# A two-layer decoder trunk: when a held feature pair's operands are made, and where the adding DMAs stand

## The chip, the cores and the metric

The kernel runs on one core of one Trainium2 chip. The metric is the device time of one execution in microseconds (us); lower is better. The program is written with a scheduler that decides the order of each engine's instructions by priorities and its own estimates, except where the code pins an instruction with `tc.keep_in_program_order`. Five engines take part: TensorE (PE, its weight loads PEld), VectorE (DVE), ScalarE (ACT), GpSimd (POOL) and the sync engine (SP). Each works its own list of instructions in order. DMAs are issued from SP's list (plain loads) and from POOL's list (loads that add to what already stands in the tile).

## The reference, cut to what matters

Two layers, each an attention mixer and a gated MLP, on a sequence of 512 tokens, width 1024, MLP width 2816 (22 features of 128):

```python
for layer in range(DEPTH):
    h = rms_norm(x, g_mix[layer])
    qkv = h @ w_in[layer]
    ...
    x = x + mix @ w_out[layer]
    h2 = rms_norm(x, g_ffn[layer])
    x = x + conv_gated_mlp(h2, w_up[layer], conv_w[layer], conv_b[layer], w_down[layer])
return rms_norm(x, g_final)

def conv_gated_mlp(h, w_up, conv_w, conv_b, w_down):
    u = causal_depthwise_conv(h @ w_up, conv_w, width=3) + conv_b
    gate, val = jnp.split(u, 2, axis=-1)
    return (jax.nn.silu(gate) * val) @ w_down
```

The change touches only the MLP's down projection, `(silu(gate) * val) @ w_down`, and what prepares its operands.

## The kernel before, in words

Every product is made of float32r parts: an operand is split into a rounded part (`whi`, cast by ACT) and the rest (`wlo`, subtracted by DVE), and PE makes three products of the parts. A list `units` (built before the layers run) names every weight tile in the order of use. `emit_dma` issues a unit's loads into raw buffers (5 of them), `emit_split` makes `whi` and `wlo` of it, and `use` hands a unit to the products and lets splits and loads run ahead as far as the buffers go.

The MLP runs over features of 128 columns. `up_pair(f)` is the gate and value up projection of feature f (PE tiles `upg` and `upv`, 24 matmuls each), followed by the convolution (ACT and DVE), SiLU and the product of the two, a page of 512 tokens. The down projection of features 0 to 17 is not made directly but by Winograd's form of Strassen's scheme, in three folds of three feature pairs each (`FOLDS`); features 18 to 21 go plainly (`PLAIN`). For that, sums and differences of both operands are needed:

- of the activations: `operands(g0, g1, qa)`, for a pair of features. Four 128x256 sums on POOL (tiles `s12` and `s34`, shown as `s`), then casts on ACT and subtractions on DVE into `ga` and `gs`.
- of `w_down`: a unit of kind `s1` loads two raw tiles `r0` and `r1` and a tile `tt` from SP, and POOL then adds further blocks of the weights by DMA: one of 256 KB onto half of `r0`, one of 512 KB onto all of `tt`, one of 256 KB onto half of `tt`. The three are issued together in `emit_dma` (L240 to L242), and the third adds onto bytes that the second has just written, so it waits for the second to land. When the unit is split, `emit_split` issues a fourth one (L277, 256 KB, onto half of `tt`), whose result is the unit of kind `s2`.

`fold(pairs)` makes the products: `p1` and `p5` of pair 0 and of pair 1 (they read `r0`), `p7` and `p6` of both (they read `tt`), then `p1`, `p6`, `p7`, `p5` of pair 2, then the products of the `s2` units, pair by pair. Each product is 6 matmuls, into the tiles `dx`, `dz`, `dw` and `dy`. So the first matmul that reads pair 2's `tt` is the first one of its `p6`, and this one comes right behind pair 2's `p1`.

Around the folds stands the loop at L1067:

```python
held = None
for f0, n in FOLDS:
    pairs = [pair_of(*held)] if held else []
    for f in range(f0 + 2 * len(pairs), f0 + n, 2):
        ...
    held = up_pair(f0 + n), up_pair(f0 + n + 1, HOLD_PRIO)
    fold(pairs)
```

The two features behind a fold (`held`) are projected before the fold, so that the fold's weights have time. Their operands (`pair_of`) are made at the head of the next fold's turn. In a layer this happens twice, behind the first and the second fold; behind the third the held features go to the plain part, which needs no such operands. Nothing pins the loads into `tt` on SP, nor the adding DMAs on POOL: their tiles are free early (three buffers, shared with a tile of attention), so the scheduler has pulled the `tt` loads and the two `tt` adds ahead, for the first fold of a layer into that layer's attention, for the other two to the end of the fold before.

Of the kernel before, what the change touches and what calls it, by code (L numbers as in the profile page):

```python
# [15 lines left out]
OP = mybir.AluOpType  # L16
# [47 lines left out]
def kernel(  # L64
# [21 lines left out]
    nc = tc.nc  # L86
# [37 lines left out]
    def bank(name, dtype=F, shape=(128, 512)):  # L124
        side = name in SIDE
        return pp.tile(list(shape), dtype, name=name, tag="side" if side else "main",
                       bufs=SIDE_BANKS if side else 8 - SIDE_BANKS)
# [80 lines left out]
    def raw_tile(shape=(128, 2, 512)):  # L208
        return sb.tile(list(shape), F, name="raw", tag="raw", bufs=RAW_BUFS)

    def emit_dma(force=False):
        u = n_dma[0]
        if u >= len(units) or (not force and n_raw[0] + RAWS[units[u][0]] > RAW_BUFS):
            return False
        n_dma[0] += 1
        kind, w, l, a, pieces = units[u]
        n_raw[0] += RAWS[kind]
        if kind == "t":
            k0, n = a
            raw = raw_tile()  # L220
            o = 0
            for c0, nc_ in pieces:
                nc.sync.dma_start(
                    out=raw[:, 0:n, o:o + nc_],
                    in_=w[l, k0 * 128:(k0 + n) * 128, c0:c0 + nc_].rearrange("(k p) c -> p k c", p=128))
                o += nc_
        elif kind == "f":
            raw = raw_tile((128, KD, 128))
            nc.sync.dma_start(out=raw, in_=w[l, :, a:a + 128].rearrange("(k p) c -> p k c", p=128))
        elif kind == "s1":  # L230
            raw = [raw_tile() for _ in range(2)]
            r0, r1 = raw
            tt = sb.tile([128, 2, 512], F, name="tt", tag="qkst", bufs=WIDE)


            b = w[l, a * 128:(a + 2) * 128, :].rearrange("(k p) (c n) -> p k c n", k=2, c=2)
            nc.sync.dma_start(out=r0, in_=b[:, 0])
            nc.sync.dma_start(out=tt, in_=b[:, 0])
            nc.sync.dma_start(out=r1, in_=b[:, 1])
            nc.gpsimd.dma_start(out=r0[:, 1], in_=b[:, 0, 0], accum_op=OP.add)  # L240
            nc.gpsimd.dma_start(out=tt, in_=b[:, :, 1], accum_op=OP.add)
            nc.gpsimd.dma_start(out=tt[:, 0], in_=b[:, 1, 1], accum_op=OP.add)  # L242
            raw = r0, r1, tt
        else:
            raw = None
        raws[u] = raw
        return True

    def hi_lo(src, shape=(128, 2, 512), n=None):
        hi = sb.tile(list(shape), FR, name="whi", tag="whi", bufs=HL_BUFS)  # L250
        lo = sb.tile(list(shape), FR, name="wlo", tag="wlo", bufs=HL_BUFS)
        n = n or shape[1]
        A.copy(hi[:, 0:n], src)
        V.tensor_tensor(out=lo[:, 0:n], in0=src, in1=hi[:, 0:n], op=OP.subtract)
        return hi, lo

    def emit_split():
        u = n_split[0]
        if u >= len(units):
            return  # L260
        while n_dma[0] <= u:
            emit_dma(True)
        n_split[0] += 1
        raw = raws.pop(u)
        kind, _, l, a, _ = units[u]
        with tc.high_priority(PRIO if u > 3 else 0):
            if kind == "t":
                split[u] = hi_lo(raw[:, 0:a[1]], n=a[1])
                n_raw[0] -= 1
            elif kind == "f":  # L270
                split[u] = hi_lo(raw, (128, KD, 128))
                n_raw[0] -= 1
            elif kind == "s1":
                r0, r1, tt = raw
                split[u] = hi_lo(r0), hi_lo(tt)

                nc.gpsimd.dma_start(out=tt[:, 0], in_=w_down[l, (a + 1) * 128:(a + 2) * 128, 0:512], accum_op=OP.add)  # L277
                kept[l, a] = r1, tt
                n_raw[0] -= 1
            else:  # L280
                r1, tt = kept.pop((l, a))
                split[u] = hi_lo(r1), hi_lo(tt[:, 0:1], n=1)
                n_raw[0] -= 1
        while emit_dma():
            pass
# [99 lines left out]
    for i, s in enumerate((lambda_q1, lambda_k1, lambda_q2, lambda_k2)):  # L385
        nc.sync.dma_start(out=lam_in[:, i, :],
                            in_=bass.AP(tensor=s.tensor, offset=s.offset, ap=[[0, 128], [1, DEPTH * 32]]))
    gd = const.tile([128, DEPTH], F, name="gd")
    for l in range(DEPTH):
        for h in range(2):  # L390
            nc.sync.dma_start(out=gd[64 * h:64 * h + 64, l:l + 1],
                                in_=g_diff[l:l + 1, :].rearrange("a p -> p a"))
# [187 lines left out]
    def act_h(k):  # L580
        return hT["hi"][k // 4][:, k % 4, :], hT["lo"][k // 4][:, k % 4, :]
# [345 lines left out]
    def mlp(l, nxt):  # L927
# [17 lines left out]
        def up_pair(f, prio=0):  # L945

            if f == 0:
                wts = use(4, 0)
                bs = [bank("up") for _ in range(4)]
                for i in range(2):  # L950
                    for g in range(4):
                        wh, wl = wts[g]
                        for k in range(KD):
                            ah, al = act_h(k)
                            sl = slice(256 * i, 256 * i + 256)
                            three_f(bs[g][:, sl], wh[:, k, :], wl[:, k, :], ah[:, sl], al[:, sl],
                                    k == 0, k == KD - 1)
                        now[0] += 2.6
                        if i == 0 and g in (1, 2):
                            hT_of(1 + g)  # L960
                        if i == 1:
                            emit_split()
                table_set(SILU)
                first.update({0: bs[0:2], 1: bs[2:4]})
            if f in first:
                bg, bv = first.pop(f)
            else:
                bg = feat_group("upg")
                bv = feat_group("upv")
            with tc.high_priority(prio):  # L970
                cg, cvl = conv((bg, bv), f)
            act(cg, cg, AF.Silu)
            V.tensor_tensor(out=cvl, in0=cg, in1=cvl, op=OP.mult)
            return cvl
# [87 lines left out]
        def pair_of(g0, g1):  # L1062
            qa = sb.tile([128, 8, 256], FR, name="ga", tag="quad", bufs=QUADS)
            parts(qa, 0, 1, g0[:, 0:256])
            return operands(g0, g1, qa)

        held = None  # L1067
        for f0, n in FOLDS:
            pairs = [pair_of(*held)] if held else []
            for f in range(f0 + 2 * len(pairs), f0 + n, 2):  # L1070
                qa = sb.tile([128, 8, 256], FR, name="ga", tag="quad", bufs=QUADS)
                g0 = up_pair(f)
                parts(qa, 0, 1, g0[:, 0:256])
                g1 = up_pair(f + 1)
                pairs.append(operands(g0, g1, qa))
            held = up_pair(f0 + n), up_pair(f0 + n + 1, HOLD_PRIO)
            fold(pairs)

        gh, gl = quad("gh"), quad("gl")
        f0, n = PLAIN  # L1080
# [120 lines left out]
```

## Time and profile before

| | |
|---|---|
| median of 3 runs | 1273.32 us (1272.75 to 1274.54) |
| the profiled execution, its own time | 1275.58 us |
| its span, first to last instruction | 1273.8 us |
| granted TensorE clock over the span, 1 is full speed | 0.991 |
| PE busy | 1220.1 us (96%), 5888 matmuls |
| DVE, ACT, POOL busy | 901.1, 672.7, 361.2 us |
| DMA: from SP's and the hardware's queue, from POOL's adding queue | 119.17 MB, 24.04 MB |

PE is busy nearly throughout, and every matmul of 512 columns starts 0.23 us after the one before when nothing is in the way. So time is read from the places where PE's next matmul starts later than that. An engine's idle time elsewhere costs nothing by itself.

### The profile page before, as it was taken

The numbers are of one execution on the slowest core, as the hardware profiler recorded it, in microseconds if no ns is written. First come the engines' busy times: TensorE is split into PE (matmuls) and PEld (weight loads), VectorE is DVE, ScalarE is ACT, GpSimd is POOL, SyncE is SP. The second block draws the span as 40 slices with busy tenths as digits, with TensorE's granted clock in tenths as the row PEclk, the third lists the DMA queues.
The fourth block names the chain that finished last, engine by engine and source line by source line (L and its number), as shares of the span: only waits on it lengthen the run. The fifth ranks groups of instructions, "written<-read, shape, count | busy, mean of one in ns | idle before, by whom it ended". The sixth has DMA issues, their size and how long they took to land. (4 is left out here: it accounts for less than half of the span.)

```text
span 1273.8 us, 16609 instructions
## 1 busy us (share of the span) xinstructions
PE 1220.1 (96%) x5888; PEld 991.7 (78%) x5888; DVE 901.1 (71%) x1619; ACT 672.7 (53%) x1224; POOL 361.2 (28%) x388
## 2 busy tenths in 40 slices
PE   6999899999999999999997999999999999999997
PEld 5877777789887887888885777878888878878885
DVE  6888878576668668568675768774776776675774
ACT  4767777544443443444463747783454444434444
POOL 3021335131125225223212114441212333332213
PEclk9999999999999999999999999999999999999999
DMA  6561112233447647745318121122244595585421
GB/s 224 159 150 50 60 58 66 69 90 93 113 107 194 153 112 177 179 100 142 97 46 207 55 82 56 61 70 67 84 116 111 136 210 122 127 205 131 99 83 67
DMA packets 157828, 144.27 MB, mean 113 GB/s; under 512 B 6826, under 2 KB 125648, under 8 KB 157744
## 3 DMA queue, kind: packets, MB, share of 16 engines
q1 hardware_dynamic: 144800, 119.17, 30.9%
q0 software_dynamic: 12944, 24.04, 11.9%
q8 instruction: 46, 0.75, 0.2%
q14 instruction: 38, 0.31, 0.1%
HBM read 141.09 MB, written 2.10 MB: 112 GB/s over the span
## 5 line engine op out<-in xcount | busy, mean ns | idle before, releaser
L99 DVE TENSOR_TENSOR wlo<-raw,whi 128x1024 fp32r<-128x1024 f32 x196 | 257.5, 1316 | 122.9 <-ACT whi L99 121.4
L99 ACT CAST whi<-raw 128x1024 fp32r<-128x1024 f32 x196 | 204.2, 1049 | 150.1 <-PE upg L99 39.6
L99 PE MATMUL upg<-hTh,whi 128*128 128x512 f32 x320 | 126.8, 396 | 6.4 <-ACT whi L99 6.4
L99 PE MATMUL upg<-hTh,wlo 128*128 128x512 f32 x320 | 127.1, 397 | 2.1 <-DVE wlo L99 2.1
L99 PE MATMUL upg<-hTl,whi 128*128 128x512 f32 x320 | 126.3, 395 | 0.0
L99 PE MATMUL upv<-hTh,whi 128*128 128x512 f32 x320 | 124.5, 389 | 0.0
L99 PE MATMUL upv<-hTl,whi 128*128 128x512 f32 x320 | 124.5, 389 | 0.0
L99 PE MATMUL upv<-hTh,wlo 128*128 128x512 f32 x320 | 124.5, 389 | 0.0
L99 POOL TENSOR_SCALAR p<-p,sm 128x512 f32<-128x512 f32 (+3 forms) x128 | 79.3, 630 | 154.1 <-PE sc L99 70.7
L99 ACT ACTIVATE p<-p,sm 128x512 f32<-128x512 f32 (+3 forms) x160 | 89.2, 559 | 45.8 <-DVE sm L99 44.7
L99 POOL TENSOR_TENSOR hn<-x,gbc 128x512 f32<-128x512 f32 x39 | 53.2, 1376 | 174.7 <-ACT hn L99 168.3
L99 PEld LDWEIGHTS upg<-hTh,whi 128*128 128x128 f32 x320 | 61.2, 191 | 20.6 <-ACT whi L99 8.1
L99 PEld LDWEIGHTS upg<-hTh,wlo 128*128 128x128 f32 x320 | 61.2, 191 | 16.6 <-DVE wlo L99 3.9
L99 ACT ACTIVATE cg<-cg 128x512 f32<-128x512 f32 x44 | 27.8, 632 | 86.4 <-DVE cg L99 86.3
L99 POOL TENSOR_TENSOR s<-cv 128x256 f32<-128x256 f32 x36 | 34.7, 982 | 135.9 <-DVE cv L99 135.9
L99 DVE TENSOR_TENSOR wlo<-tt,whi 128x1024 fp32r<-128x1024 f32 (+1 forms) x36 | 45.0, 1251 | 39.4 <-ACT whi L99 39.2
L99 PEld LDWEIGHTS upg<-hTl,whi 128*128 128x128 f32 x320 | 61.2, 191 | 12.9
L99 PEld LDWEIGHTS upv<-hTh,whi 128*128 128x128 f32 x320 | 60.1, 188 | 12.5
L99 PEld LDWEIGHTS upv<-hTl,whi 128*128 128x128 f32 x320 | 60.1, 188 | 12.5
L99 PEld LDWEIGHTS upv<-hTh,wlo 128*128 128x128 f32 x320 | 60.0, 188 | 12.5
L99 DVE SCALAR_TENSOR_TENSOR cv<-upv,conv,cv 128x511 f32<-128x511 f32 x80 | 59.7, 746 | 1.4
L99 DVE SCALAR_TENSOR_TENSOR cg<-upg,conv,cg 128x511 f32<-128x511 f32 x80 | 59.7, 746 | 1.4
(234 smaller groups left out, 3104.2 us busy)
## 6 DMA issues: line engine op xcount, KB each, us to landing
raw<-in_w_up_dram SPq DMA_DIRECT2D x88, 512.0 KB, 4.0
raw<-in_w_down_dram SPq DMA_DIRECT2D x44, 512.0 KB, 4.3
raw<-in_w_in_dram SPq DMA_DIRECT2D x40, 512.0 KB, 3.9
tt<-in_w_down_dram SPq DMA_DIRECT2D x18, 512.0 KB, 4.6
tt<-in_w_down_dram POOLq DMA_DIRECT2D x18, 512.0 KB, 9.1
tt<-in_w_down_dram POOLq DMA_DIRECT2D x36, 256.0 KB, 4.1
raw<-in_w_out_dram SPq DMA_DIRECT2D x16, 512.0 KB, 3.5
raw<-in_w_down_dram POOLq DMA_DIRECT2D x18, 256.0 KB, 4.1
```

What stands on the lines that cost most here:

```text
L99: i = f(*a, **k)
```

## The change

Three edits, all in the MLP's preparation.

1. The held pair's operands are made one step later: behind the up projection of the next fold's first own feature, not ahead of it. The loop covers the same features.
2. The load of `tt` on SP is kept in program order, so it stands between the loads of `r0` and `r1` of its unit.
3. The adding DMAs are no longer issued in `emit_dma`. They are put on a list in two stages for each unit, the first with the adds onto `r0` and onto all of `tt`, the second with the add onto half of `tt`. Each later `emit_split` issues one stage, and all stages that the unit to be split still needs. All adding DMAs, the fourth one too, are kept in program order on POOL.

```diff
             nc.sync.dma_start(out=r0, in_=b[:, 0])
-            nc.sync.dma_start(out=tt, in_=b[:, 0])
+            tc.keep_in_program_order(nc.sync.dma_start(out=tt, in_=b[:, 0]))
             nc.sync.dma_start(out=r1, in_=b[:, 1])
-            nc.gpsimd.dma_start(out=r0[:, 1], in_=b[:, 0, 0], accum_op=OP.add)
-            nc.gpsimd.dma_start(out=tt, in_=b[:, :, 1], accum_op=OP.add)
-            nc.gpsimd.dma_start(out=tt[:, 0], in_=b[:, 1, 1], accum_op=OP.add)
+            adding.append((u, [(r0[:, 1], b[:, 0, 0]), (tt, b[:, :, 1])]))
+            adding.append((u, [(tt[:, 0], b[:, 1, 1])]))
...
+    def add_now(dst, src):
+        tc.keep_in_program_order(nc.gpsimd.dma_start(out=dst, in_=src, accum_op=OP.add))
+
+    def add_some(u):
+
+        some = True
+        while adding and (some or adding[0][0] <= u):
+            some = False
+            for dst, src in adding.popleft()[1]:
+                add_now(dst, src)
...
         n_split[0] += 1
+        add_some(u)
         raw = raws.pop(u)
...
-                nc.gpsimd.dma_start(out=tt[:, 0], in_=w_down[l, (a + 1) * 128:(a + 2) * 128, 0:512], accum_op=OP.add)
+                add_now(tt[:, 0], w_down[l, (a + 1) * 128:(a + 2) * 128, 0:512])
...
         for f0, n in FOLDS:
-            pairs = [pair_of(*held)] if held else []
-            for f in range(f0 + 2 * len(pairs), f0 + n, 2):
+            pairs = []
+            for f in range(f0 + (2 if held else 0), f0 + n, 2):
+                g0 = up_pair(f)
+                if held:
+                    pairs.append(pair_of(*held))
+                    held = None
                 qa = sb.tile([128, 8, 256], FR, name="ga", tag="quad", bufs=QUADS)
-                g0 = up_pair(f)
                 parts(qa, 0, 1, g0[:, 0:256])
```

What the three edits do to the lists of two engines is shown here for the first fold of the first layer; the other folds read alike. The tiles are numbered by this order: `raw_3393` and `tt_3395` are the first unit's, `raw_3483` and `tt_3485` the second's, `raw_3565` and `tt_3567` the third's.

POOL's list before, from the first unit's add to the first sum behind the fold's products (the adds onto `tt_3395`, `tt_3485` and `tt_3567` from L241 and L242 stand far above, in attention):

```order
L240 DMA raw_3393<-in_w_down_dram 128x512
L240 DMA raw_3483<-in_w_down_dram 128x512
L99 TENSOR_TENSOR s12_3466<-cv_3456,cv_3377 128x256
L99 TENSOR_TENSOR s34_3467<-cv_3377 128x256
L99 TENSOR_TENSOR s12_3466<-s12_3466,cv_3377 128x256
L99 TENSOR_TENSOR s34_3467<-s12_3466,cv_3456 128x256
L240 DMA raw_3565<-in_w_down_dram 128x512
L277 DMA tt_3395<-in_w_down_dram 128x512
L277 DMA tt_3485<-in_w_down_dram 128x512
L277 DMA tt_3567<-in_w_down_dram 128x512
L99 TENSOR_TENSOR dt_3751<-du_3747,x2_0_68 128x512
```

And POOL's list after the change, from the last two of the third pair's four sums on (ahead of those sums stand the first unit's two first-stage adds, onto `raw_3393` and `tt_3395`):

```order
L99 TENSOR_TENSOR s12_3465<-s12_3465,cv_3376 128x256
L99 TENSOR_TENSOR s34_3466<-s12_3465,cv_3455 128x256
L251 DMA tt_3395<-in_w_down_dram 128x512
L251 DMA raw_3483<-in_w_down_dram 128x512
L251 DMA tt_3485<-in_w_down_dram 128x2x512
L251 DMA tt_3485<-in_w_down_dram 128x512
L251 DMA tt_3395<-in_w_down_dram 128x512
L251 DMA raw_3565<-in_w_down_dram 128x512
L251 DMA tt_3567<-in_w_down_dram 128x2x512
L251 DMA tt_3485<-in_w_down_dram 128x512
L251 DMA tt_3567<-in_w_down_dram 128x512 x2
```

Six `tt` adds (three of 512 KB and three of 256 KB) have come into the run-up to the fold, and all the adds but two now stand behind the third pair's sums. The second `tt_3395` row here and the second 128x512 row of `tt_3485` are the fourth adds of their units; of the two in the last row the first completes the third unit's `tt`, and the second is its fourth add.

ACT's list at the end of a fold, as a piece of the difference (`gs` is the held pair's, `whi<-raw` are the weights of the up projections that follow):

```order
 L99 CAST ga<-cv 128x512
 L99 CAST whi<-tt 128x512
-L99 CAST gs<-s_3857 128x512
-L99 CAST gs<-s_3858 128x512
 L99 CAST whi<-raw 128x1024 x5
 L99 ACTIVATE cg<-upg,conv 128x512
```

The two casts of the held pair's sums have left their place ahead of the five weight casts; they now stand behind the next value projection's `cv` activation. PE's list is the same in the whole MLP; in the second layer's attention a few `vab` and `vc` matmuls have changed places with those of the scores.

## Rows read from the trace of the kernel before

**Rows 1.** The page, its first line.

```profile
span 1273.8 us, 16609 instructions
```

**Rows 2.** PE's timeline, end of layer 2's second fold: start us, us, engine, what, [idle before <-releaser].

```profile
1121.89 0.39 PE L99 MATMUL dz<-whi,gs 128*128 128x512 f32 x1
1123.86 0.50 PE L99 MATMUL upg<-hTh,whi 128*128 128x512 f32 x1 [1.58 <-ACT whi L99]
...
1125.12 0.80 PE L99 MATMUL upg<-hTh,wlo 128*128 128x512 f32 x1 [0.53 <-DVE wlo L99]
...
1131.82 0.39 PE L99 MATMUL upv<-hTh,whi 128*128 128x512 f32 x1
```

**Rows 3.** PE's timeline, end of layer 2's third fold.

```profile
1220.43 0.39 PE L99 MATMUL dz<-whi,gs 128*128 128x512 f32 x1
1220.65 0.39 PE L99 MATMUL upg<-hTh,whi 128*128 128x512 f32 x1
```

**Rows 4.** PE's timeline, end of each layer's first fold.

```profile
397.96 0.39 PE L99 MATMUL dz<-whi,gs 128*128 128x512 f32 x1
...
407.91 0.39 PE L99 MATMUL upv<-hTh,whi 128*128 128x512 f32 x1
...
1024.88 0.39 PE L99 MATMUL dz<-whi,gs 128*128 128x512 f32 x1
...
1033.28 0.39 PE L99 MATMUL upv<-hTh,whi 128*128 128x512 f32 x1
```

**Rows 5.** ACT's timeline, end of layer 2's second fold.

```profile
1122.25 0.62 ACT L99 CAST gs<-s 128x512 fp32r<-128x512 f32 x1 [2.54 <-POOL s L99]
1122.77 3.88 ACT L99 CAST whi<-raw 128x1024 fp32r<-128x1024 f32 x4
```

**Rows 6.** Windows: us; busy (x instructions) of PE, PEld, DVE, ACT, POOL; PEclk, DMA, GB/s.

```profile
1121.00:1132.00 11.00, 8.89 (x31) 6.60 (x30) 10.62 (x12) 4.61 (x6) 3.35 (x4) 0.84 0.75 161
```

**Rows 7.** PE's timeline, the start of layer 2's attention.

```profile
691.23 0.44 PE L99 MATMUL sc<-sk,sq 128*128 128x384 f32 x1 [4.77 <-DVE sm L99]
...
698.84 0.58 PE L99 MATMUL sc<-sk,sq 128*128 128x256 f32 x1 [4.19 <-DVE sm L99]
```

**Rows 8.** POOL's timeline, the same place; L241 adds 512 KB, L242 256 KB.

```profile
685.85 0.90 POOL L242 DMA_DIRECT2D tt<-in_w_down_dram  x1 [5.89 <-DMA tt<-in_w_down_dram]
686.95 2.43 POOL L241 DMA_DIRECT2D tt<-in_w_down_dram  x2 [0.19 <-issue]
688.44 1.67 POOL L99 TENSOR_SCALAR p<-p,sm 128x512 f32<-128x512 f32 x1
695.33 0.90 POOL L242 DMA_DIRECT2D tt<-in_w_down_dram  x1 [5.21 <-DMA tt<-in_w_down_dram]
...
697.87 0.89 POOL L242 DMA_DIRECT2D tt<-in_w_down_dram  x1 [0.56 <-DMA tt<-in_w_down_dram]
```

**Rows 9.** Windows from the first `vab` to the first `op` matmul, layer 1 and layer 2.

```profile
44.55:221.54 176.99, 168.50 (x881) 131.40 (x880) 147.54 (x400) 127.69 (x286) 55.52 (x74) 1.00 0.34 93
668.66:848.47 179.81, 167.80 (x850) 129.94 (x850) 129.59 (x348) 119.39 (x273) 55.93 (x74) 0.98 0.33 91
```

**Rows 10.** POOL's timeline, run-up to layer 2's second fold.

```profile
1077.86 1.56 POOL L99 TENSOR_TENSOR s<-s,cv 128x256 f32<-128x256 f32 x2
1079.36 0.87 POOL L240 DMA_DIRECT2D raw<-in_w_down_dram  x1
```

**Rows 11.** POOL's timeline, `tt` adds in layer 2's up projections.

```profile
1021.99 1.22 POOL L241 DMA_DIRECT2D tt<-in_w_down_dram  x1
...
1029.91 0.90 POOL L242 DMA_DIRECT2D tt<-in_w_down_dram  x1 [4.68 <-DMA tt<-in_w_down_dram]
...
1041.17 0.91 POOL L242 DMA_DIRECT2D tt<-in_w_down_dram  x1 [9.12 <-DMA tt<-in_w_down_dram]
```

**Rows 12.** POOL's three L277 adds (256 KB) of layer 2's second fold, 1075 to 1110 us.

```profile
DMA to landing us min/median/max: 4.0/4.1/4.1
```

**Rows 13.** ACT's timeline, the third unit's `tt` in layer 2's second fold.

```profile
1098.76 1.05 ACT L99 CAST whi<-tt 128x1024 fp32r<-128x1024 f32 x1 [1.66 <-PE dz L99]
```

**Rows 14.** DVE's timeline, the same tile.

```profile
1099.85 1.22 DVE L99 TENSOR_TENSOR wlo<-tt,whi 128x1024 fp32r<-128x1024 f32 x1 [1.14 <-ACT whi L99]
```

**Rows 15.** PE's timeline, second matmul of pair 2's `p6`, layer 2's second fold.

```profile
1105.59 0.39 PE L99 MATMUL dy<-wlo,gs 128*128 128x512 f32 x1
```

More of the change, by code (lines that the diff above doesn't have):

```diff
@@ L247, in emit_dma @@
         return True
+    adding = deque()
+    def add_now(dst, src):
[6 more added lines that the diff above has]
+                add_now(dst, src)
     def hi_lo(src, shape=(128, 2, 512), n=None):
```

## The prediction, before the changed kernel was run

> **What bounds the kernel now.** PE does. I read the page first, then PE's timeline at each place where a matmul starts late, then the timelines of the engines that it waited for there, and last POOL's list of adding DMAs. The profiled execution took 1275.58 us around a span of 1273.8 [rows 1], 2.26 above the median of the runs, 1273.32; sums are made against 1275.58, and 2.26 comes off at the end. A measurement tells about 0.2% from no change, 2.5 us.
>
> In the MLP, PE is late in one kind of place that costs much: the end of the first and the second fold of each layer. The last matmul of the fold starts at 1121.89, and the value projection behind it at 1131.82 [rows 2], 9.93 us later. Where nothing is in the way, the next matmul comes after 0.22 us [rows 3], and 24 gate matmuls and the step before them take 25 x 0.227 = 5.67. So 4.26 are lost. Of these, 1.58 and 0.53 are shown as idle [rows 2], waiting for the first `whi` and `wlo`; the other 2.15 are matmuls at half pace, since the granted clock there is 0.84 on average over the 11 us [rows 6], with the lower of the two levels, 1.2 GHz, behind the idle time. ACT shows the cause: the weight casts begin at 1122.77, right behind the held pair's second `gs` cast, which had waited 2.54 for POOL's sums [rows 5]. The layer's first fold ends in the same way: 407.91 - 397.96 - 5.67 = 4.28 in layer 1, and 1033.28 - 1024.88 - 5.67 = 2.73 in layer 2 [rows 4], where the clock did not fall. The second fold of layer 1 reads as the 4.28 one. The third folds lose nothing [rows 3]: they have no held operands behind them.
>
> The other place is layer 2's attention: PE waits 4.77 and 4.19 us for DVE [rows 7]. DVE waits there for POOL's scaling of the scores (`p`), and POOL stood behind hoisted `tt` adds, from 685.85 to 688.44, and again until 695.33 [rows 8].
>
> **The change, part by part.**
>
> *Held operands later.* The `gs` casts leave the front of the weight casts. The third folds show what is left then: nothing. Gain 4.28 + 4.28 + 2.73 + 4.26 = 15.6. The moved work (four sums, their casts and subtractions) lies beside the next up projections, and its products are wanted a fold later; ACT and DVE have idle time in those 10.9 us of PE work. I cost it at nothing. If that cover failed, one `gs` cast of 0.62 [rows 5] ahead of a weight cast would be the size of it.
>
> *`tt` loads and adds out of attention.* At most this gives the 8.96 us of idle time [rows 7] and what the lower clock took behind it; the granted clock of the stretch is 0.98 over 179.81 us [rows 9], so 7 us at 1.2 GHz, some 3 us lost: 12. At least it gives what layer 2 needs more than layer 1 for the same stretch, 179.81 - 176.99 = 2.8 [rows 9]; layer 1 even has 31 more small transposes in it. Waits that PE did not meet in layer 2 because it was late will come back: layer 1 has 176.99 - 168.50 = 8.5 idle, layer 2 12.0. I take 5.5, near the low end, because layer 1 is the nearest row to a layer 2 without the big stall. The few matmuls that changed places there I cost at nothing, since they are the same matmuls.
>
> *`tt` loads in order on SP.* Three loads of 512 KB for each fold go from one busy stretch to another. SP has waited for raw buffers there, not for the DMAs. Nothing.
>
> *The adds in two stages, in order on POOL.* This is where the time goes back. Before, when the run-up to a fold began, `tt` was ready but for its fourth add, and POOL's only add behind the third pair's sums, ahead of the fourth ones, was the one of 256 KB at 1079.36 [rows 10]. Now from 1079.36 on POOL must issue, in this order: the first unit's second stage (256 KB), the second unit's two first-stage adds (256 and 512), and only when the 512 has landed its second stage; then a fourth add, then the third unit's two first-stage adds (256 and 512), and only when this 512 has landed its last 256. POOL's list stops at each of these waits. PE wants the third unit's `tt` at the second matmul of pair 2's `p6`, 1105.59 [rows 15]: 26.2 us after 1079.36. (The first fold of a layer has about as much.)
>
> How long the chain takes, from rows of adds in a row:
> - 256 and then 512 KB: from issue to the next waiting issue 695.33 - 685.85 = 9.48 [rows 8]. A further 512 KB behind it came 697.87 - 695.33 = 2.54 later, so another 256 costs 1.27. The first part, 256 + 256 + 512: 9.48 + 1.27 = 10.75.
> - The second part is 256 + 256 + 256 + 512 KB, as many bytes as the 256 + 512 + 512 that took 697.87 - 685.85 = 12.02 [rows 8].
> - The last 256: 4.1 to land [rows 12].
> - Cast and subtraction: 1.05 and 1.22, from 1098.76 to 1101.07 [rows 13, 14]: 2.3.
>
> Together 10.75 + 12.02 + 4.1 + 2.3 = 29.2, so PE waits 29.2 - 26.2 = 3.0 us at each `p6`. The bounds: if an add is not held up by those ahead of it in the queue, a 512 needs 1029.91 - 1021.99 = 7.9 [rows 11] behind the issue of the others, some 0.7 each, and the chain is (1.4 + 7.9) + (2.1 + 7.9) + 4.0 + 2.3 = 25.6: no wait, with 0.6 to spare. If plain loads run beside it as they do in the up projections, a 256 and a 512 take 1041.17 - 1029.91 = 11.26 [rows 11], and the chain is 12.5 + 13.8 + 4.1 + 2.3 = 32.7: 6.5 us of wait. I take 3.0: the adds of rows 8 had few loads beside them, like the run-up to a fold, and they did queue behind each other.
>
> The second unit's `tt` lands at about 1079.36 + 10.75 + 4.1 = 1094.2 and is split by 1096.5; its first matmul, in `p7`, stands 19 matmuls ahead of the one at 1105.59, at 1105.59 - 19 x 0.227 = 1101.3, so that is covered. Behind the waiting cast of the third `tt` stand on ACT the casts of the `s2` units and the copies of `dx`; they move with PE, which needs them 4 us later, so I add nothing.
>
> To a wait comes what the clock takes. Behind the idle 2.1 of rows 2 it was 2.15, behind the same idle time in layer 2's first fold 0.6. I take 1.5. Six folds: 6 x (3.0 + 1.5) = 27.0.
>
> **The sum.** 27.0 - 15.6 - 5.5 = +5.9: 1281.5 on the profiled execution's scale, 1279.2 on the median's, slower by 0.5%.
>
> **Rivals.**
>
> *The adds land in time.* Then only the gains are left: -21.1, 1252.2 (from 1246 to 1255 with attention's bounds). For it: the low chain of 25.6 just fits. Against it: the adds of rows 8 plainly queued. The Trainium skill, page "DMA: Bandwidth & Descriptors", section "Anatomy of one DMA — SWDGE (gpsimd) path", gives about 2 us and the bytes at 436 GB/s for a DMA from POOL, which would be 2.6 for 256 KB and 3.2 for 512 KB, an estimate from that page; by it this rival would hold with room, and the time would be near 1252. This case's trace does not agree for adds: 4.1 [rows 12] and 7.9 [rows 11].
>
> *A short wait.* The wait is 1 us, and the clock falls only behind some of them (0.8 on average): 6 x 1.8 - 21.1 = -10.3, 1263.0. It needs a chain of 27.2, 2 us less than mine; loads beside the adds speak against it, fewer waits for the clock speak for it.
>
> *A long wait.* Plain loads slow the adds as in the up projections, 6.5 us and 2.15 for the clock: 6 x 8.65 - 21.1 = +30.8, 1304.1. From a chain of about 31 on, the second unit's `tt` is late too, and the value convolution behind it on ACT holds up `dy`. For it: the third load of a unit and one up weight lie beside the chain. Against it: in the up projections there are five or six such loads.
>
> The side of zero turns where 6 x (wait + clock) is 21.1, so at 3.5 us for each fold, with my clock at a wait of 2.0, a chain of 28.2.
>
> **How the numbers follow.** My forecast, waits of 2 to 4.5 us (1273 to 1289), gets 0.50, of which 0.08 falls within 0.2%; in time 0.20; a short wait 0.20, with 0.04 within 0.2%; a long wait 0.10. Faster by over 0.2%: 0.20 + 0.16 = 0.36; within: 0.12; slower: 0.42 + 0.10 = 0.52. The forecast's own range is 1273 to 1289. The range for 8 in 10, 1256 to 1294, takes the forecast and the short wait whole, and the near edges of the other two.
>
> **What would show it.** Right: no idle time of PE ahead of `upg` at the ends of the folds; at pair 2's `p6` PE idle before `dy` on ACT's `whi` or DVE's `wlo`, six times, about 3 us each; ACT's cast of the third `tt` released by a DMA; POOL's waits for `tt` landings standing in the run-up to the folds; attention in layer 2 without the two long waits. Wrong: `dx` going over to `dy` without a gap (the adds are quicker than rows 8 say), the fold ends still late (another wait was behind the `gs` casts), or a new wait at the second unit's `p7`.

## The result: slower by 1.5%, and the profile after

The changed kernel takes 1291.73 us (median of 4 runs, 1290.71 to 1295.07) against 1273.27 (4 runs, 1272.75 to 1274.54) on the same chip: a ratio of 1.0148 [1.0128, 1.0168], 18.5 us slower where the forecast was 5.9 slower. The time lies in the range given, near its upper end. The profiled execution took 1290.71 us around a span of 1288.9, 15.1 us above the one before [rows 1]. It is the fastest of the four, and the profiled one before stood 2.3 us above its median, so the spans differ by less than the medians.

```profile
span 1288.9 us, 16627 instructions
```

First the gains. PE's timeline at the end of layer 2's second fold, now without any wait:

```profile
1131.97 0.39 PE L99 MATMUL dz<-whi,gs 128*128 128x512 f32 x1
1132.20 0.39 PE L99 MATMUL upg<-hTh,whi 128*128 128x512 f32 x1
```

It reads as [rows 3]; the other three places do too, so the 15.6 us of [rows 2, 4] are gone, as forecast. The windows from the first `vab` to the first `op` matmul, layer 1 and layer 2 (columns as in [rows 6]), answer to [rows 9]:

```profile
43.63:218.85 175.22, 168.08 (x881) 131.59 (x880) 147.45 (x400) 127.33 (x286) 48.48 (x68) 1.00 0.23 71
679.12:847.61 168.49, 164.63 (x851) 128.43 (x850) 129.29 (x348) 119.41 (x273) 49.59 (x68) 1.00 0.23 74
```

That is 1.8 us less in layer 1 and 11.3 in layer 2: 13.1, where 5.5 was forecast. The loss is in the folds. The waits of PE that are new or grown (in us: total, times, longest):

```profile
PE dw L99 <- DVE cv L99: 11.4, 6, 2.4
...
PE dy L99 <- ACT whi L99: 10.4, 6, 3.3
...
PE dy L99 <- DVE wlo L99: 4.4, 6, 0.8
PE dz L99 <- DVE dv L99: 4.2, 6, 0.8
```

Each comes six times, once in a fold. PE's timeline in layer 2's second fold, its first matmul and the three late ones:

```profile
1096.73 0.39 PE L99 MATMUL dx<-whi,ga 128*128 128x512 f32 x1
...
1105.43 0.47 PE L99 MATMUL dw<-whi,gs 128*128 128x512 f32 x1 [2.42 <-DVE cv L99]
...
1113.61 0.50 PE L99 MATMUL dy<-whi,gs 128*128 128x512 f32 x1 [0.22 <-ACT whi L99]
1114.87 0.49 PE L99 MATMUL dy<-wlo,gs 128*128 128x512 f32 x1 [0.76 <-DVE wlo L99]
```

The second `dy` matmul of pair 2 stands 55 matmuls behind the fold's first one, 12.47 us without a wait. Before, in all six folds, it came exactly then; the fold that ends in [rows 2] began here, 12.47 us ahead of [rows 15]:

```profile
1093.12 0.39 PE L99 MATMUL dx<-whi,ga 128*128 128x512 f32 x1
```

After the change it comes 1114.87 - 1096.73 = 18.14 us behind: 5.67 late. Over the six folds it is 17.8 to 18.9, on average 18.34: **5.87 us late, where the forecast had 3.0**. A whole fold, from its first `dx` to the next `upg`, takes 35.2 to 38.3 us, on average 36.5; undisturbed it takes 29.0 (before: 28.99 in layer 2's third fold). So the adds cost 7.5 us for each fold, 45.0 in all, where the forecast had 27.0. POOL's timeline shows the chain (L251 issues every add):

```profile
1083.02 0.88 POOL L251 DMA_DIRECT2D tt<-in_w_down_dram  x1
1083.60 1.17 POOL L251 DMA_DIRECT2D raw<-in_w_down_dram  x1
1084.14 1.88 POOL L251 DMA_DIRECT2D tt<-in_w_down_dram  x1
1095.28 1.79 POOL L251 DMA_DIRECT2D tt<-in_w_down_dram  x2 [9.27 <-DMA tt<-in_w_down_dram]
1096.43 1.51 POOL L251 DMA_DIRECT2D raw<-in_w_down_dram  x1
1097.13 2.04 POOL L251 DMA_DIRECT2D tt<-in_w_down_dram  x1
1104.20 0.89 POOL L251 DMA_DIRECT2D tt<-in_w_down_dram  x1 [5.03 <-DVE wlo L99]
1106.86 0.88 POOL L251 DMA_DIRECT2D tt<-in_w_down_dram  x1 [1.77 <-DMA tt<-in_w_down_dram]
```

From the first unit's second stage (1083.02) to the second unit's (1095.28) 12.26, from there to the third's (1106.86) 11.58, and 5.65 more until ACT casts the third `tt`. Over the six folds the three parts are 11.98, 11.67 and 5.87 on average. ACT's timeline, the casts of the second and third unit's `tt` and what stands behind the first of them:

```profile
1101.53 1.05 ACT L99 CAST whi<-tt 128x1024 fp32r<-128x1024 f32 x1 [4.60 <-DMA tt<-in_w_down_dram]
1102.49 0.77 ACT L99 ACTIVATE cv<-upv,conv 128x512 f32<-128x512 f32 x1
...
1112.51 1.05 ACT L99 CAST whi<-tt 128x1024 fp32r<-128x1024 f32 x1 [7.36 <-DMA tt<-in_w_down_dram]
```

The second unit's `tt` is late as well, and the convolution of the held value (`cv`) waits behind its cast on ACT, then behind its subtraction (`wlo`) on DVE:

```profile
1102.62 1.22 DVE L99 TENSOR_TENSOR wlo<-tt,whi 128x1024 fp32r<-128x1024 f32 x1 [6.41 <-ACT whi L99]
1103.76 1.53 DVE L99 SCALAR_TENSOR_TENSOR cv<-upv,conv,cv 128x511 f32<-128x511 f32 x2
```

That value projection stands in a PSUM bank of the same group (`SIDE`) as `dw`, so the fold's second `dw` bank is free only when `cv` is done: the wait of 2.42 us at 1105.43.

### The profile page after: what moved, and what is told of

Same layout as the page of the kernel before. It is cut to its first block, busy times and chain, and to the rows that moved or that the text cites. A ratio compares the mean times of both kernels' runs of the same rounds, so it can differ in the third digit from the quotient of the medians.

```text
span 1288.9 us, 16627 instructions
## 1 busy us (share of the span) xinstructions
PE 1224.6 (95%) x5888; PEld 993.7 (77%) x5888; DVE 892.7 (69%) x1619; ACT 670.3 (52%) x1224; POOL 366.2 (28%) x388
## 3 DMA queue, kind: packets, MB, share of 16 engines
q0 software_dynamic: 12944, 24.04, 11.5%
## 5 line engine op out<-in xcount | busy, mean ns | idle before, releaser
L99 DVE TENSOR_TENSOR wlo<-raw,whi 128x1024 fp32r<-128x1024 f32 x196 | 262.2, 1339 | 118.3 <-ACT whi L99 117.3
L99 PE MATMUL upg<-hTh,wlo 128*128 128x512 f32 x320 | 124.5, 389 | 0.0
L251 POOL DMA_DIRECT2D tt<-in_w_down_dram x54 | 64.3, 1223 | 140.9 <-DVE wlo L99 73.5
L99 ACT CAST whi<-tt 128x1024 fp32r<-128x1024 f32 (+1 forms) x36 | 29.9, 831 | 77.8 <-DMA tt<-in_w_down_dram 71.7
```

The costliest lines, as they stand in the source:

```text
L99: i = f(*a, **k)
L251: tc.keep_in_program_order(nc.gpsimd.dma_start(out=dst, in_=src, accum_op=OP.add))
```

## The experiments

Two theories stood for the loss. **T1**: one chain of adds, from the third pair's sums to the third unit's `tt`, sets the time; the wait at `dw` lies inside it. **T2**: the waits at `dw` and `dy` are separate and add up. And the forecast's split of the gains was open. All ratios are to the kernel before, on the same chip. "Attention alone", the two "spread" runs and "fourth adds later" ran on a chip where the kernel before takes 1275.6 us, the others where it takes 1273.3 to 1273.7; across the two chips, ratios are compared. The mean fold is that of the one profiled execution, from the first `dx` matmul to the next `upg`.

| run | median us | ratio [95%] | mean fold us |
|---|---|---|---|
| before | 1273.3 to 1275.6 | 1 | 30.2 |
| the change | 1291.73 | 1.0148 [1.0128, 1.0168] | 36.5 |
| held edit alone | 1286.64 | 1.0096 [1.0063, 1.0130] | 33.8 |
| without the held edit | 1293.88 | 1.0159 [1.0134, 1.0183] | 36.4 |
| convolution first | 1296.84 | 1.0176 [1.0154, 1.0197] | 37.3 |
| two stages at once | 1290.30 | 1.0125 [1.0101, 1.0148] | 36.3 |
| fourth adds later | 1280.00 | 1.0041 [1.0027, 1.0055] | 35.0 |
| the last three edits together | 1282.31 | 1.0080 [1.0050, 1.0111] | 34.9 |
| attention alone | 1260.51 | 0.9895 [0.9869, 0.9921] | 30.2 |
| loads in order alone | 1267.43 | 0.9958 [0.9939, 0.9977] | 33.0 |
| held edit and loads in order | 1263.69 | 0.9936 [0.9907, 0.9964] | 31.8 |
| spread, held edit | 1246.29 | 0.9779 [0.9758, 0.9799] | 29.0 |
| spread, no held edit | 1249.68 | 0.9802 [0.9784, 0.9821] | 29.0 |

### The change taken apart

**The held edit alone**: the loop of the change in the kernel before, nothing else.

> The kernel before with edit 1 alone: the held pair's operands one step later; loads and adds of tt as before. Theory A (the prediction's term taken alone: the moved work is covered): PE loses nothing at the ends of the first and second folds, nothing else moves, 1273.3 - 15.6 = 1257.7 us (range 1253 to 1262). Theory B (the parts need each other): in this order POOL's list has the held pair's four sums behind all six early tt adds, the last of which is issued in the kernel before at 1051.28 us, 26.4 us after the fold's last matmul at 1024.88; ACT's gs casts stand behind the sums and ahead of the weight casts for the next features, so PE runs dry about 22 us behind the fold's end and waits 4.5 to 10 us, at four places: 1273.3 - 15.6 + 18 to 40 = 1276 to 1298 us.

1286.64 us, inside theory B's span and 13 us slower than before, but the wait is elsewhere than B had it. The ends of the folds are clear: 5.67 us from the last `dz` matmul to the first `upv`, at all four, so edit 1 by itself does bring the 15.6 us of the forecast. More than that is lost inside the folds: the second and third fold of each layer take 35.3 to 36.9 us, 29.0 more in all than undisturbed ones. ACT's timeline, then SP's, then PE's in layer 2's second fold:

```profile
1058.70 0.62 ACT L99 CAST gs<-s 128x512 fp32r<-128x512 f32 x1 [13.68 <-POOL s L99]
```

```profile
1080.46 0.33 SPq L237 DMA_DIRECT2D raw<-in_w_down_dram  x1
```

```profile
1102.71 0.60 PE L99 MATMUL dx<-whi,ga 128*128 128x512 f32 x1 [2.11 <-ACT whi L99]
1105.66 0.80 PE L99 MATMUL dx<-wlo,ga 128*128 128x512 f32 x1 [2.35 <-DVE wlo L99]
```

The held sums stand behind all six `tt` adds and their waits, and ACT stands 13.68 us before the first `gs` cast. PE has weights for longer than that, so it doesn't run dry. But the casts behind free raw buffers late, SP issues the second unit's `r0` load late (1080.46, 17.3 us ahead of the fold's first matmul at 1097.72; before, 1064.59 and 28.5), and PE waits for that unit in the fold, at pair 1's `dx`, four times.

**Without the held edit**: the changed kernel with the loop as it was before.

> The changed kernel with edit 1 undone: tt loads and adds in program order, held operands where they were before. Theory A (the terms add up): the 15.6 us at the four fold ends come back, 1291.7 + 15.6 = 1307.3 us (1303 to 1311), attention stays as in the changed kernel. Theory B (POOL, now free of early tt adds at the folds' ends, makes the held sums sooner, so the old loss is smaller): 1295 to 1302 us.

1293.88 us: only 2.2 above the change, less than either theory had and within the spread of the two kernels' runs. The ends of the folds are short without the held edit too: 5.67 us at three of them, 6.48 at the fourth. ACT's timeline at the end of layer 2's first fold in the kernel before, and then in this run:

```profile
1022.08 0.62 ACT L99 CAST gs<-s 128x512 fp32r<-128x512 f32 x1 [4.33 <-POOL s L99]
1025.26 0.62 ACT L99 CAST gs<-s 128x512 fp32r<-128x512 f32 x1 [2.56 <-POOL s L99]
```

```profile
1029.51 0.62 ACT L99 CAST gs<-s 128x512 fp32r<-128x512 f32 x1 [4.27 <-POOL s L99]
1030.34 0.62 ACT L99 CAST gs<-s 128x512 fp32r<-128x512 f32 x1 [0.20 <-POOL s L99]
```

Before, a hoisted `tt` add (1021.99, [rows 11]) and a sum onto `x` stood on POOL ahead of the last held sum. With the adds gone, the scheduler puts the four held sums together and the second cast waits 0.20. So nearly all of the 15.6 us comes with edits 2 and 3 alone, and all of it came with edit 1 alone: they remove the same wait, and beside the other two, edit 1 adds little.

### The chain

**Convolution first**: in the changed kernel the cast and the subtraction of the second unit's `tt` are made to stand behind the held value's convolution.

```diff
-        A.copy(hi[:, 0:n], src)
-        V.tensor_tensor(out=lo[:, 0:n], in0=src, in1=hi[:, 0:n], op=OP.subtract)
+        c = A.copy(hi[:, 0:n], src)
+        d = V.tensor_tensor(out=lo[:, 0:n], in0=src, in1=hi[:, 0:n], op=OP.subtract)
+        if after:
+            behind(c, after[0])
+            behind(d, after[1])
...
```

> The changed kernel with one order turned round on ACT and on DVE, at all six folds: the held value's convolution stands ahead of the cast and the subtraction of the second unit's tt. PE's wait before the second dw bank (11.4 us of idle time over six folds, and about 1.5 us at half pace behind each) must go. Theory T1 (the end of the chain of adds sets the time): the third unit's tt lands when it did, the idle time moves to dy, and the time stays within 4 us of the changed kernel: 1288 to 1293 us. Theory T2 (the waits stand for themselves and add up): 6 x (1.9 + 1.5) = 20 us come back, 1271 us (1268 to 1276).

1296.84 us: no gain, T2 falls. The wait at `dw` is gone from PE's waits, and the one at `dy` has taken it up:

```profile
PE dy L99 <- ACT whi L99: 28.9, 6, 6.3
...
PE dy L99 <- DVE wlo L99: 3.1, 6, 0.8
```

The second `dy` matmul comes 18.49 us behind the fold's first on average; with the wait at `dw` in place it was 18.34. The 5 us more are of another kind. The windows of layer 2's second fold in the changed kernel and in this run (columns as above):

```profile
1096.73:1132.20 35.47, 31.28 (x127) 24.57 (x126) 23.07 (x23) 13.80 (x18) 19.95 (x16) 0.95 0.61 130
```

```profile
1100.99:1138.90 37.91, 31.88 (x127) 25.16 (x126) 24.35 (x25) 13.70 (x17) 18.91 (x15) 0.91 0.59 126
```

A granted clock of 0.95 over 35.47 us is 3.5 us at 1.2 GHz, 0.91 over 37.91 is 6.8. In this fold of the changed kernel the low clock lay behind the `dw` wait, ahead of the late `dy`, where PE had to wait anyway; the matmuls stand 0.43 apart there:

```profile
1106.41 0.63 PE L99 MATMUL dy<-whi,gs 128*128 128x512 f32 x1
1106.84 0.63 PE L99 MATMUL dy<-wlo,gs 128*128 128x512 f32 x1
```

In the convolution run it lies behind the late `dy`, where nothing hides it. This fold shows the contrast at its largest, 2.4 us. Over the six folds of the changed kernel the slow stretch lies ahead of that `dy` in three, behind it in two, and in one there is none; in the convolution run it lies behind it in all six, and the mean fold is 0.8 us longer.

**Two stages at once**: each split issues two stages of the list, so that the first unit's second stage stands ahead of the third pair's sums.

```diff
-        some = True
+        some = 2
         while adding and (some or adding[0][0] <= u):
-            some = False
+            some = max(some - 1, 0)
```

> The changed kernel, but each split issues two stages of the list of adds, not one: the first unit's second stage (256 KB) stands ahead of the third pair's sums and out of the run-up; everything else keeps its order. Theory T1 (the chain of adds behind the sums is bound by the bytes in it and sets the time): the chain is one add of 256 KB shorter, about 1.3 us at each of six folds, and some of the clock: 1291.7 - 8 to 12 = 1280 to 1284 us. Theory T3 (each stage costs its own latency, bytes hardly matter): only the issue of that add goes, 0.6 us each, 1287 to 1290 us.

1290.30 us, 1.4 less, which is within the spread of the two kernels' runs. POOL's timeline in layer 2's second fold, the first add behind the sums and the second unit's second stage:

```profile
1085.36 0.84 POOL L251 DMA_DIRECT2D raw<-in_w_down_dram  x1
1096.27 1.79 POOL L251 DMA_DIRECT2D tt<-in_w_down_dram  x2 [8.81 <-DMA tt<-in_w_down_dram]
```

That is 10.91 us where it was 12.26, so one add of 256 KB in the queue is 1.35 (1.4 on average over the six folds), as T1 has it. But `dy` came only 1.0 us earlier on average (0.2 to 1.8), and a fold is only 0.2 shorter: the slow stretch lies behind the late `dy` in five of six folds here, in two of six in the changed kernel. T1's size was wrong, and T3's reason (0.6 us of issue) as well.

**Fourth adds later**: in the changed kernel the fourth adds of units 1 and 2 are issued behind the third unit's second stage.

```diff
-                add_now(tt[:, 0], w_down[l, (a + 1) * 128:(a + 2) * 128, 0:512])
+                fourth.append((tt[:, 0], w_down[l, (a + 1) * 128:(a + 2) * 128, 0:512]))
+                while len(fourth) and a % 6 == 4:
+                    add_now(*fourth.popleft())
...
```

> The changed kernel with the fourth adds (256 KB) of the first and the second unit behind the third unit's second stage, so that the chain from the third pair's sums to the third unit's tt has one add of 256 KB less in it, and no add is issued closely ahead of its last one. Theory T1 (the chain sets the time and queued bytes count): 1.3 us shorter by the bytes and 1.5 us by a last add that lands in 4.1 and not 5.6 us, and PE's wait at dy falls by that at six folds: 1291.7 - 17 = 1275 us (1271 to 1280). Theory T4 (the chain gains, but the fourth adds are then late for the s2 units, or the clock takes what is gained): 1285 to 1295 us.

1280.00 us, 11.7 less by the medians and 13.6 by the ratios, at the upper edge of T1's range. `dy` comes 16.77 us behind the fold's first matmul, 1.57 earlier, and a fold is 1.5 shorter. It is the largest gain of a single edit to the chain. The third unit's second stage and the two fourth adds now stand in a row on POOL, and ACT casts the third `tt` 4.69 us behind:

```profile
1101.55 2.68 POOL L252 DMA_DIRECT2D tt<-in_w_down_dram  x3 [8.22 <-DMA tt<-in_w_down_dram]
1106.24 1.05 ACT L99 CAST whi<-tt 128x1024 fp32r<-128x1024 f32 x1 [6.91 <-DMA tt<-in_w_down_dram]
```

Over the six folds the chain is 2.0 us shorter on average, where T1 had 2.8: the last add 1.1 (T1: 1.5), the part before it 0.7 (T1: 1.3), the rest in the first part. Four folds keep a granted clock of 1.00; in the changed kernel one does. In the last fold T1 does not hold: the wait at `dw` (3.5 us, with a slow stretch behind it) sets the time there, not the chain's end.

**The last three together**:

> The changed kernel with the edits of three runs before together: the first unit's second stage ahead of the third pair's sums, the fourth adds of units 1 and 2 behind the third unit's second stage, the held value's convolution ahead of the second unit's tt. Theory T1 (one chain, from the third pair's sums to the third unit's tt, sets the time): from the sums to that tt's cast 29.5 us in the changed kernel, 1.35 less by the first edit, 2.3 less by the second, none by the third, so 25.8, with cast and subtraction 28.1 against PE's lead of 26.2: a wait of 1.9 us and about 1.5 of clock and follow-up, 3.4 at six folds where it was 7.9: 1291.7 - 27 = 1265 us (1260 to 1270). Theory T2 (waits at dw, dy and dz are separate): the value convolution's wait goes too and the time is near 1255 us. If the single edits' gains simply add (+5.1, -1.4, -11.7): 1284 us.

1282.31 us, near what the single gains add up to (1284 by the medians, 1280 by the ratios) and not T1's 1265; by the ratios it is no better than the run before. `dy` comes at 16.01 us, 2.33 earlier than in the changed kernel and not some 4. In layer 2's second fold the chain's first two parts take 10.91 and 10.46 us, 2.5 less than before these edits, but the last add, with two others right behind it, took 6.7 us to ACT's cast, where the run before had 4.7 with the same three adds issued in a row. Over the six folds it is 4.2 to 6.7 here, and 4.0 to 4.7 in five folds and 6.7 in one there. What makes that difference stays open. The clock took the rest: `dy` is 0.8 us earlier than in the run before, but the slow stretch lies behind it in five of six folds, where the run before has it there in one, and the mean fold is as long.

### The gains, and the adds elsewhere

**Attention alone**: in the kernel before, the three `tt` loads of each layer's first fold and their adds stand, in program order, at the head of the up projections.

```diff
...
+            keep(nc.sync.dma_start(out=tt, in_=b[:, 0]))
+            keep(nc.gpsimd.dma_start(out=tt, in_=b[:, :, 1], accum_op=OP.add))
+            keep(nc.gpsimd.dma_start(out=tt[:, 0], in_=b[:, 1, 1], accum_op=OP.add))
...
             if f == 0:
+                tt_early(l)
                 wts = use(4, 0)
...
```

> The kernel before with one thing changed: the three tt loads of each layer's first fold and their two adds each stand, in program order, at the head of that layer's up projections, not in its attention. Held operands and the other folds as before. This prices the attention term alone. The prediction's term: 1273.3 - 5.5 = 1267.8 us. By the traces of before and of the changed kernel (first value projection to first output projection: layer 2 179.8 to 168.5, layer 1 177.0 to 175.2): 1273.3 - 13.1 = 1260.2 us (1257 to 1263). A rival, that six adds and their waits on POOL at the head of the up projections hold up the first pair's sums: above 1270 us.

1260.51 us, 1.05% or 13.4 us below the kernel before on that chip, as the traces had it. The same two windows:

```profile
43.44:218.65 175.21, 168.05 (x882) 131.51 (x880) 147.41 (x400) 127.34 (x286) 48.53 (x68) 1.00 0.24 72
665.52:833.99 168.47, 164.67 (x851) 128.41 (x850) 129.48 (x348) 119.38 (x273) 49.35 (x68) 1.00 0.24 74
```

**Spread**: the held edit, and the `tt` loads and adds of every fold pinned into its up projections: those of the first fold at the head of the layer, the others one or two at a time behind each pair's sums.

```diff
...
                 if held:
                     pairs.append(pair_of(*held))
                     held = None
+                    tt_early(l, f0)
+                    add_some(1)
+                elif f0:
+                    add_some(2)
...
                 pairs.append(operands(g0, g1, qa))
+                if f0:
+                    add_some(2 if f == f0 + 2 else 1)
...
```

> The held pair's operands one step later as in the change, but all tt loads and tt adds pinned into the up projections, behind the held pair's sums, one waiting add between the sums of one pair and the next: neither in attention, nor at the ends of the folds, nor in the run-up. Theory A (the changed kernel's loss is the chain of adds in the run-up and nothing else; both gains are real): no waits on tt at dw and dy, 1273.3 - 15.6 - 13.1 = 1244.6 us (1241 to 1249). Theory B (the adds cost time wherever they stand, since they slow the loads of the weights or hold up POOL's sums as in the run with the held edit alone): 1255 us or more.

1246.29 us, theory A: 2.2% faster than before, and the fastest of all. No wait of PE on `dw`, `dy` or `upg` is left; all six folds take 29.0 us at full clock. Layer 2's second fold:

```profile
1067.85:1096.85 29.00, 28.86 (x127) 23.58 (x126) 23.06 (x23) 13.92 (x17) 16.69 (x12) 1.00 0.38 93
```

The same adds, 24.04 MB of them in the whole kernel, cost PE nothing that shows here.

**Spread, no held edit**: the same with the held operands at their old place.

> As the run before, but the held pair's operands at their old place, ahead of the next up projection. Theory C (the loss at the ends of the folds came from an early tt add and another sum that stood on POOL among the held pair's sums; without them edit 1 is worth nothing): within 4 us of the run before, about 1245 to 1249 us. Theory D (the gs casts ahead of the weight casts cost the time, as the prediction has it): 15.6 us more than the run before, about 1260 us.

1249.68 us, theory C. What the `gs` casts cost there by themselves is 3.4 us: a wait of about 0.6 for `wlo` at each of four ends, each of which is 0.88 us longer.

**Loads in order alone**: the kernel before with edit 2, one line; the adds follow their loads, but the scheduler places them.

```diff
-            nc.sync.dma_start(out=tt, in_=b[:, 0])
+            tc.keep_in_program_order(nc.sync.dma_start(out=tt, in_=b[:, 0]))
```

> The kernel before with edit 2 alone: tt loads in program order on SP; the adds as before, three for each unit together and not pinned. In this order POOL's list has the first two units' adds, with both waits for landing, ahead of the third pair's sums, and only the third unit's behind them. Theory A (what costs in the changed kernel is that the staged list puts two waits for landing behind the third pair's sums): the chain behind the sums is 256 + 512 + 256 KB, some 10 + 5 us and 2.3 for the splits, well inside the lead of 26 us; attention's 13 and most of the fold ends' 15 us are gained; but the third pair's sums wait for the second unit's tt, about 6 us, which may cost up to 3 us at each fold: 1246 to 1263 us. Theory B (any tt load and add in the run-up costs, staged or not): 1275 us or more.

1267.43 us (median of 10 runs, 1263.05 to 1273.87; the profiled one is the slowest), faster than before and 24 us below the change, but above theory A's span. The ends of the folds take 6.55 to 6.60 us, so this one line brings 12 of the 15.6 us. The chain behind the sums is short, yet the third pair's sums wait for the second unit's 512 KB add. POOL's timeline, then ACT's:

```profile
1075.24 0.90 POOL L242 DMA_DIRECT2D tt<-in_w_down_dram  x1 [9.18 <-DMA tt<-in_w_down_dram]
1075.84 1.76 POOL L99 TENSOR_TENSOR s<-cv 128x256 f32<-128x256 f32 x2
```

```profile
1078.32 0.62 ACT L99 CAST gs<-s 128x512 fp32r<-128x512 f32 x1 [8.57 <-POOL s L99]
```

ACT loses 8.57 us there, the held features' convolutions come late, and PE waits at `dw` again:

```profile
PE dw L99 <- DVE cv L99: 13.5, 6, 2.4
```

**Held edit and loads in order**: the change without its staged list.

> The kernel before with edits 1 and 2, without edit 3: the changed kernel with the adds issued together again. Theory A: as the run before less what the gs casts still cost there: 0 to 4 us below it. Theory B: the held edit needs the staged adds, since its sums stand behind waits for landing as in the run with edit 1 alone: above the run before by 5 us or more.

1263.69 us (median of 7, 1259.88 to 1271.90), 3.7 below the run before and so on theory A's side. The two spreads overlap, but the ends of the folds are back at 5.67 us, 3.6 us less in all four. Of the waits of the change only the one at `dw` is left, none at `dy`:

```profile
PE dw L99 <- DVE cv L99: 11.1, 6, 2.4
```

So edits 1 and 2 together are faster than the kernel before by 0.64%, and it is edit 3 that turns them into a loss: 28 us between this run and the change. Edit 3 puts two waits for landing behind the third pair's sums, and fourth adds among them; "fourth adds later" prices the place of the fourth adds at 11.7 to 13.6 of the 28, and no run prices the two waits by themselves.

## Why the prediction was right or wrong

The side was right, and so was the place of the wait (ACT's cast of the third `tt`, released by a DMA, six times) and its cause, the chain that POOL issues behind the third pair's sums. The size was wrong: 18.5 us for 5.9.

- *"The adds in two stages ... so PE waits 29.2 - 26.2 = 3.0 us at each `p6`."* **This is the step that failed.** The lead was right: 55 matmuls behind a start 13.7 us after the sums. The chain was too short: 12.26 + 11.58 + 5.65 and 2.36 for cast and subtraction are 31.85 in place of 29.2, and the wait 5.87 on average in place of 3.0, near the upper bound of 6.5 that the text had worked out and set aside. The first part was 1.5 us longer than its sum of rows (1.2 on average over the six folds), the last add 1.55 longer than the 4.1 of [rows 12] (1.8 on average), the second part 0.4 shorter. In the first part the step of 1.27 for 256 KB more was right (1.35 in the run with two stages at once). Its base was not: 256 and 512 KB took 10.91 us there (10.2 to 11.3 over the six folds), not the 9.48 of [rows 8]; the 11.26 of [rows 11], kept for the bound because plain loads lay beside it, was the nearer row. Whether plain loads are the reason no run shows.
- *"I take 1.5"* for the clock: a fold is 7.5 us longer than undisturbed, of which 5.87 is the wait, so 1.6 for the clock and the waits at `dz`. The size is right, but 0.7 of it is the wait at `dz`, behind work that the text took to move with PE at no cost. What the clock takes depends on where the slow stretch falls, as the convolution run shows.
- *"The second unit's `tt` lands at about ... 1094.2 ... so that is covered."* For its own matmul this held; for what stands behind it, not. It was cast 18.5 us behind the chain's start (1101.53 - 1083.02), where the text had it land after 14.8, and its subtraction ended at 1103.84, ahead of 1104.9, when its matmul was due without a wait. But the value convolution behind it freed a `dw` bank too late. The forecast put that convolution into the long-wait rival, at `dy`; it came at `dw`, and the convolution run shows that in the changed kernel this wait cost nothing by itself: it lies inside the chain.
- *"Held operands later ... Gain ... 15.6."* The sum was right, and moving the `gs` casts does clear the ends. But the text took the wait for POOL's sums as given: it came from a `tt` add and another sum that stood among the held sums, and edits 2 and 3 clear the ends without edit 1. With the adds away from the held sums edit 1 is worth 2 to 4 us, in three pairs of runs; alone it clears the ends and makes the kernel 13 us slower, since the held sums then stand behind the adds.
- *"I take 5.5, near the low end"* for attention: 13.1 by the windows, 1.05% [0.79, 1.31] by the run alone. Layer 1 was taken as the floor for layer 2, but layer 1 paid 1.8 us itself, and layer 2, which has 30 fewer matmuls there, needs 168.5 without the adds.

With the measured terms the sum closes: 45.0 - 15.6 - 13.1 = +16.3, and the spans differ by 15.1. Two errors of opposite sign, +18.0 and -7.6, hid each other in part; that the time still lies in the stated range is partly luck. Of the rivals, "a long wait" had the mechanism nearest to what happened, at 0.10.

## What to carry to other kernels

An instruction list that stops at each landing makes a chain out of DMAs that could overlap: where a staged order is written out by hand, lay out the chain from the last free point to the consumer, with every add in it, and put the waits where the engine has nothing else to do. The same adds cost 45 us in the run-up to the folds and nothing between the up projections. And before a gain is put down to one edit of several, look at what else stands in the waiting engine's list: here two edits each removed the same wait, and the gain was booked to the one that, beside the other, is worth 2 to 4 us.

## What the runs showed of the hardware

- Here a wait cost more in one piece at the end than in two: with nearly the same time to `dy` (18.34 and 18.49 us), taking the earlier wait away made the mean fold 0.8 us longer, since the half-pace stretch (1.2 GHz) then lay behind the last wait in all six folds, not in two. In layer 2's second fold the granted clock went from 0.95 to 0.91.
- Adding DMAs from POOL slow one another: 256 KB more ahead of a 256 and a 512 KB add is 1.35 us until the latter lands, and the last add of 256 KB, issued 2.7 to 3.6 us behind another, landed 5.6 to 6.1 us behind its issue over the six folds, where those of [rows 12], with no other add under way, landed in 4.1. How much of that the other add makes is open: in the kernel before, an add of 256 KB at 1051.28, with no other add under way but with plain loads beside it (149 GB/s in all), took 5.9.
